# The front's adaLN weight blocks are loaded from GpSimd's queue instead of SyncE's

## The chip, the cores and the metric

The kernel runs on one core of a Trainium2 chip. The metric is the device time of one execution in microseconds (us). A core has TensorE (PE, with its weight loads PEld), VectorE (DVE), ScalarE (ACT), GpSimd (POOL) and SyncE (SP), which here only issues DMAs. Each engine takes its instructions in a fixed order and waits where one isn't ready.

## What is computed

One decoder layer over 256 tokens of width 2048. From a conditioning vector c a modulation is computed, a product of silu(c) with a weight of 2048 x 12288. It gives six vectors of 2048: shift, scale and gate for each of two sub-layers.

```
c_act = silu(c)
mod = c_act @ w_ada + b_ada
sh1, sc1, g1, sh2, sc2, g2 = split(mod, 6)
h = layer_norm(x) * (1 + sc1) + sh1
mix = token_mix(h, ...)          # one input projection w_in, two kinds of attention, w_o
x = layer_norm(alpha * x + g1 * mix)
h = layer_norm(x) * (1 + sc2) + sh2
ffn = peer(h, ...)               # queries w_pq, product keys, tables u and v
x = layer_norm(alpha * x + g2 * ffn)
```

## The kernel before, in words

Activations are kept transposed, 128 channels on the partitions, in 16 chunks. Weights come as pieces of 1 MB (128 partitions x 4 x 512 floats), 32 of w_in, then w_uq, w_uk, w_uv, 16 of w_o, 16 of w_pq, then the tables u and v. Some pieces are multiplied as they are, in float32 (L334); most are first split into a high and a low part: ACT casts the high part (L101), DVE subtracts it for the low part (L103), and PE makes three products (L140 to L142).

The modulation isn't a matmul. `ada` (L207) loads one block of w_ada, 1 MB, which holds the weights of 128 outputs, and DVE multiplies its two halves with the broadcast silu(c) and sums along the rows (L212, some 1.2 us each). The block's number j says which 128 of the 12288 outputs it gives. After a group of blocks `ada_bias` (L215) adds the two halves and the bias; ACT then applies shift and scale (L305, L740). The front, everything up to the table phase, takes 80 blocks this way:

- Eight blocks (shift and scale of the first four chunks) come before the first w_in piece can be finished. `group_start` (L359) loads the small w_kr tile (kw) and modulates the four chunks in two halves. The pieces of w_in for one group of four chunks are 8; `w_in_pieces` (L315) takes the first three together, first the products with the first half of the chunks for each piece, then those with the second half.
- Between the pieces of a group, `ada_in` (L350) takes the eight blocks of the next group. Buffers: two of `front` (tag "ada"), and the tiles xt0 and xt1 that held x. For the first group, the third and fourth block lie in the buffers of the pools early_a and early_b, the fifth and sixth in xt0 and xt1, which come free once PE has transposed the normalised x.
- w_in's own pieces use a ring of three buffers of `stream` and, by turns, the ones of early_a and early_b (RAW_RING, L324). So the third piece needs the fourth block's buffer and the fifth piece the third block's.
- The other 48 blocks (gate 1, shift 2, scale 2) are pulled from a generator, `ada_rest` (L244), at places written by hand (PULLS, PULL_WO, PULL_PQ; the rest at L792), and use the two buffers of `front` alone. The last ones feed `to_h2` (L736), which the last pieces of w_pq need.

The last 16 blocks (gate 2) are loaded in the table phase by code of their own, with SP's queue (g2w).

All DMAs are issued by SP, and SP's order is the program's: an issue that waits until its buffer is free holds back all that stand behind it. The order on the other engines is planned when the program is built, from the program's order and from what is ready; semaphores are added then. GpSimd does nothing after four memsets at the start.

Of the kernel before, what the change touches and what calls it, by code (L numbers as in the profile page):

```python
# [64 lines left out]
def tile_hybrid_peer_block(ctx: ExitStack, tc: tile.TileContext, a, out):  # L65
    nc = tc.nc
# [140 lines left out]
    def ada(pool, tag, bufs, j):  # L207

        w = pool.tile([P, D], F32, tag=tag, name=f"ada{j}", bufs=bufs).rearrange("p (z n) -> p z n", z=2)
        nc.sync.dma_start(w, a["w_ada"][j].rearrange("p (z n) -> p z n", z=2))  # L210
        for z in range(2):
            nc.vector.scalar_tensor_tensor(w[:, z, :], w[:, z, :], 1.0, cb[:, z * 1024:(z + 1) * 1024], op0=ALU.mult,  # L212
                                           op1=ALU.mult, accum_out=(modc, modh)[z][:, j:j + 1])
# [29 lines left out]
    with tc.tile_pool(name="front", bufs=1) as front:  # L243
        def ada_rest():  # L244
            for j in range(G1, SH2):
                ada(front, "ada", 2, j)
                yield
            ada_bias(G1, 16)
            for kg in range(4):
                for i in range(4):  # L250
                    for j0 in (SH2, SC2):
                        ada(front, "ada", 2, j0 + 4 * kg + i)
                        yield
                for j0 in (SH2, SC2):
                    ada_bias(j0 + 4 * kg, 4)
# [20 lines left out]
        with tc.tile_pool(name="mix", bufs=1) as mix, ExitStack() as attn_pool:  # L276
# [73 lines left out]
            def ada_in(kg, m):  # L350
                j = (SH1, SC1)[m % 2] + 4 * kg + m // 2
                where = (m // 2 % 2) if kg else (0, 2, 1, 0)[m // 2]
                if where == 0:
                    return ada(front, "ada", 2, j)
                if where == 1:
                    return ada(mix, f"xt{m % 2}", 1, j)
                return ada((early_a, early_b)[m % 2], "raw", 1, j)
# [273 lines left out]
        with tc.tile_pool(name="res", bufs=1) as res:  # L631
# [16 lines left out]
            for step in range(12):  # L648
# [6 lines left out]
                n = WO_ORDER[step][0]  # L655
# [145 lines left out]
    with tc.tile_pool(name="back", bufs=1) as back:  # L801
# [218 lines left out]
        with tc.tile_pool(name="val", bufs=1) as val:  # L1020
# [28 lines left out]
            for j, c in enumerate(V_ORDER):  # L1049
# [14 lines left out]
                if 2 <= j < 18:  # L1064
                    m = G2 + j - 2
                    w = g2w[:, j % 4, :].rearrange("p (z n) -> p z n", z=2)
# [36 lines left out]
            for th in range(2):  # L1103
# [18 lines left out]
                z = stream.tile([P, 4, 512], F32, tag="raw", name=f"fin_z{th}", bufs=3)  # L1122
# [79 lines left out]
```

## Time and profile before

| what | value |
|---|---|
| time, median of 3 runs | 2034.66 us (2030.68 to 2037.2) |
| profiled execution, its own time | 2032.56 us |
| its span, first to last instruction | 2030.5 us |
| mean granted TensorE clock over the span | 0.987 |
| PE, DVE, ACT, POOL busy | 1971.3, 1487.4, 1045.6, 0.2 us |

The profile is of one execution. A share of busy time is an average over stages. A wait is put down to what ended it. A DMA's time to landing runs from its issue until its data have arrived, and includes the time that it stands behind others in its queue.

### The profile page before, as it was taken

How to read it: one execution, taken by the hardware profiler on the slowest of the kernel's cores; microseconds unless marked ns; L12 is line 12 of the kernel's file. 1: busy time of each engine (PE TensorE's matmuls, PEld its weight loads, DVE VectorE, ACT ScalarE, POOL GpSimd, SP SyncE). 2: the span in 40 equal slices, each digit the busy share in tenths (PEclk: the TensorE clock that was granted, in tenths of full speed). 3: DMA queues.
4: the chain of work that ended last, by engine and by line, in shares of the span. 5: the costliest groups of instructions: out<-in, count | busy, mean ns of one | idle time of the engine just before them, and what ended most of it. 6: DMA issues, size and time to landing. Idle time of an engine off the chain costs nothing.

```text
span 2030.5 us, 26302 instructions
## 1 busy us (share of the span) xinstructions
PE 1971.3 (97%) x10119; PEld 1645.9 (81%) x10120; DVE 1487.4 (73%) x2334; ACT 1045.6 (51%) x1536; POOL 0.2 (0%) x4
## 2 busy tenths in 40 slices
PE   6999998999999999999999999999999999999997
PEld 4567676779988888888888888888888788888886
DVE  7588987888799777677777766686776666564457
ACT  2333457535545665677777765444444344444451
POOL 0000000000000000000000000000000000000000
PEclk7999998999999999999999999999999999999999
DMA  8887887877545676677777669989999988865552
GB/s 355 335 334 306 303 326 270 342 293 296 205 168 200 225 257 249 230 265 267 274 272 283 260 244 308 330 329 327 331 339 324 295 304 280 284 220 202 188 211 98
DMA packets 142829, 554.81 MB, mean 273 GB/s; under 512 B 10864, under 2 KB 77552, under 8 KB 84848
## 3 DMA queue, kind: packets, MB, share of 16 engines
q1 hardware_dynamic: 142704, 553.14, 74.0%
q8 instruction: 79, 1.29, 0.2%
q14 instruction: 46, 0.38, 0.1%
HBM read 502.76 MB, written 50.34 MB: 272 GB/s over the span
## 4 chain that ended last, share of the span: by engine, by line
PE 86%; DVE 8%; DMA 3%; ACT 2%; issue 1%; SPq 0%; DVEq 0%; ACTq 0%
PE u_ps L135 21%; PE u_ps L136 11%; PE v_ps L141 11%; PE v_ps L140 11%; PE v_ps L142 11%; PE win_ps L334 3%; PE win_ps L141 2%; DVE ada L212 2%; PE win_ps L142 2%; PE g_ps L967 2%; PE win_ps L140 1%; PE wo_ps L142 1%; PE wo_ps L141 1%; PE wo_ps L140 1%; PE wpq_ps L762 1%; DMA gl<-g_d 1%
## 5 line engine op out<-in xcount | busy, mean ns | idle before, releaser
L135 PE MATMUL u_ps<-act,hi_u 128*128 128x512 f32 x2048 | 719.7, 395 | 0.0
L136 PE MATMUL u_ps<-act,lo_u 128*128 128x256 f32 x2048 | 574.7, 281 | 0.5 <-DVE lo_u L103 0.4
L135 PEld LDWEIGHTS u_ps<-act,hi_u 128*128 128x128 f32 x2048 | 384.2, 188 | 86.1
L101 ACT CAST hi_v<-raw_v 128x1024 fp32r<-128x1024 f32 x244 | 256.9, 1054 | 332.0 <-PE v_ps L142 302.8
L103 DVE TENSOR_TENSOR lo_v<-raw_v,hi_v 128x1024 fp32r<-128x1024 f32 x244 | 296.0, 1222 | 177.9 <-ACT hi_v L101 177.9
L103 DVE TENSOR_TENSOR lo_u<-raw_u,hi_u 128x1024 fp32r<-128x1024 f32 x256 | 312.3, 1221 | 135.7 <-ACT hi_u L101 134.9
L136 PEld LDWEIGHTS u_ps<-act,lo_u 128*128 128x128 f32 x2048 | 386.8, 189 | 2.4 <-DVE lo_u L103 2.2
L141 PE MATMUL v_ps<-lo_v,whi 128*128 128x512 f32 x976 | 379.8, 389 | 1.8 <-DVE lo_v L103 1.8
L140 PE MATMUL v_ps<-hi_v,whi 128*128 128x512 f32 x976 | 379.9, 389 | 0.5 <-DVE W L823 0.5
L142 PE MATMUL v_ps<-hi_v,wlo 128*128 128x512 f32 x976 | 379.7, 389 | 0.0
L101 ACT CAST hi_u<-raw_u 128x1024 fp32r<-128x1024 f32 x256 | 267.4, 1048 | 174.2 <-PE u_ps L135 163.0
L141 PEld LDWEIGHTS v_ps<-lo_v,whi 128*128 128x128 f32 x976 | 183.2, 188 | 39.9 <-DVE lo_v L103 2.2
L140 PEld LDWEIGHTS v_ps<-hi_v,whi 128*128 128x128 f32 x976 | 183.2, 188 | 39.2 <-DVE W L823 1.2
L142 PEld LDWEIGHTS v_ps<-hi_v,wlo 128*128 128x128 f32 x976 | 183.2, 188 | 38.3
L212 DVE SCALAR_TENSOR_TENSOR ada<-ada,cb 128x1024 f32<-128x1024 f32 x160 | 191.0, 1218 | 8.1 <-DMA ada<-in_w_ada_dram 7.9
L962 DVE TENSOR_TENSOR o<-eq,gT 128x1024 fp32r<-128x1024 f32 x64 | 78.3, 1223 | 32.7 <-PE g_ps L967 32.7
L334 PE MATMUL win_ps<-raw_win,hmod 128*128 128x512 f32 x192 | 86.4, 605 | 1.2 <-ACT hmod L305 1.2
L824 ACT ACTIVATE W<-W 128x512 f32<-128x512 f32 x64 | 40.8, 637 | 70.3 <-DVE W L823 70.3
L970 ACT COPY stg<-g_ps 128x512 f32<-128x512 f32 x128 | 72.2, 623 | 0.0
L101 ACT CAST hi_win<-raw_win 128x1024 fp32r<-128x1024 f32 x40 | 40.7, 1049 | 60.7 <-DMA raw_win<-in_w_in_dram 30.6
L334 PEld LDWEIGHTS win_ps<-raw_win,hmod 128*128 128x128 f32 x192 | 36.6, 195 | 43.3 <-issue 41.2
L141 PE MATMUL win_ps<-lo_win,act 128*128 128x512 f32 x160 | 64.0, 400 | 5.8 <-DVE lo_win L103 5.6
(340 smaller groups left out, 2411.0 us busy)
## 6 DMA issues: line engine op xcount, KB each, us to landing
raw_u<-in_u_dram SPq DMA_DIRECT2D x128, 1024.0 KB, 5.3
raw_v<-in_v_dram SPq DMA_DIRECT2D x122, 1024.0 KB, 6.2
ada<-in_w_ada_dram SPq DMA_DIRECT2D x80, 1024.0 KB, 6.7
raw_win<-in_w_in_dram SPq DMA_DIRECT2D x32, 1024.0 KB, 8.8
g_d<-stg SPq DMA_DIRECT2D x16, 2048.0 KB, 7.2
gl<-g_d SPq DMA_DIRECT2D x32, 1024.0 KB, 10.0
raw_wo<-in_w_o_dram SPq DMA_DIRECT2D x16, 1024.0 KB, 6.9
g2w<-in_w_ada_dram SPq DMA_DIRECT2D x16, 1024.0 KB, 8.1
```

The costliest lines, as they stand in the source:

```text
L101: nc.scalar.copy(hi, raw[:, 2 * j:2 * j + 2, :])
L103: nc.vector.tensor_sub(lo, raw[:, 2 * j:2 * j + 2, :], hi.bitcast(F32))
L135: nc.tensor.matmul(pss[e], hi[:, i, es], act[:, k], start=first and j == 0 and i == 0, stop=False)
L136: nc.tensor.matmul(pss[e][:, 1], lo[:, i, es], act_hi[:, k, :], start=False, stop=last and j == 1 and i == 3)
L140: nc.tensor.matmul(o, sh, mh, start=start, stop=False)
L141: nc.tensor.matmul(o, sh, ml, start=False, stop=False)
L142: nc.tensor.matmul(o, sl, mh, start=False, stop=stop)
L212: nc.vector.scalar_tensor_tensor(w[:, z, :], w[:, z, :], 1.0, cb[:, z * 1024:(z + 1) * 1024], op0=ALU.mult, op1=ALU.mult, accum_out=(modc, ...
L334: nc.tensor.matmul(ps[th], act[:, i, ts], src[:, i, :], start=i == 0, stop=i == 3)
L824: nc.scalar.activation(ws, ws, AF.Gelu)
L962: nc.vector.tensor_mul(o2, eq.unsqueeze(2).broadcast_to(both), gT[:, four, :].bitcast(F32).unsqueeze(3).broadcast_to(both))
L970: nc.scalar.copy(stg[:, :, :, t:t + 2], ps.rearrange("p (t z i) -> p z i t", t=2, z=2))
```

## The change

`ada` issues its load from GpSimd's queue. Buffers, products, the places where blocks are taken, and every other load stay. It concerns the 80 blocks of the front.

```
@@ -207,7 +207,7 @@
     def ada(pool, tag, bufs, j):
 
         w = pool.tile([P, D], F32, tag=tag, name=f"ada{j}", bufs=bufs).rearrange("p (z n) -> p z n", z=2)
-        nc.sync.dma_start(w, a["w_ada"][j].rearrange("p (z n) -> p z n", z=2))
+        nc.gpsimd.dma_start(w, a["w_ada"][j].rearrange("p (z n) -> p z n", z=2))
         for z in range(2):
             nc.vector.scalar_tensor_tensor(w[:, z, :], w[:, z, :], 1.0, cb[:, z * 1024:(z + 1) * 1024], op0=ALU.mult,
                                            op1=ALU.mult, accum_out=(modc, modh)[z][:, j:j + 1])
```

## Rows read from the trace of the kernel before

**Rows 1.** The page's first part: busy us (share of the span) and instructions.

```profile
PE 1971.3 (97%) x10119; PEld 1645.9 (81%) x10120; DVE 1487.4 (73%) x2334; ACT 1045.6 (51%) x1536; POOL 0.2 (0%) x4
```

**Rows 2.** Busy us of PE, PEld, DVE, ACT, POOL by stretch; PEclk, DMA share, GB/s.

```profile
0.00:550.00 550.00, 506.11 (x2532) 393.24 (x2534) 448.18 (x944) 246.69 (x411) 0.20 (x4) 0.96 0.78 309
550.00:2030.50 1480.50, 1465.18 (x7590) 1252.67 (x7588) 1039.26 (x1392) 798.92 (x1125) 0.00 (x0) 1.00 0.73 260
```

**Rows 3.** PE's waits, 0 to 550 us: for whom, total us, times, longest us.

```profile
PE win_ps L141 <- DVE lo_win L103: 5.6, 4, 2.9
...
PE wpq_ps L140 <- ACT hi_wpq L101: 1.3, 1, 1.3
...
PE wpq_ps L142 <- DVE lo_wpq L103: 0.9, 2, 0.5
```

**Rows 4.** PE's timeline, 0 to 46 us: start, us, operation, [idle before it and releaser].

```profile
29.59 7.13 PE L334 MATMUL win_ps<-raw_win,hmod 128*128 128x512 f32 x16 [1.17 <-ACT hmod L305]
38.65 1.10 PE L310 MATMUL kr_ps<-kw,hmod 128*128 128x64 f32 x8 [1.93 <-DMA kw<-in_w_kr_dram]
42.03 1.12 PE L310 MATMUL kr_ps<-kw,hmod 128*128 128x64 f32 x4 [2.27 <-ACT hmod L305]
```

**Rows 5.** SP's longest wait by sum, and its issues of w_ada (ns min/median/max).

```profile
SPq L210 <- DVE ada L212: 131.9, 33, 11.6
...
L210 SPq DMA_DIRECT2D ada<-in_w_ada_dram x80: 327/328/835, 2.6 to 502.8; - x80
```

**Rows 6.** SP's timeline, 0 to 48 us.

```profile
24.79 4.94 SPq L210 DMA_DIRECT2D ada<-in_w_ada_dram  x4
29.77 0.73 SPq L362 DMA_DIRECT2D kw<-in_w_kr_dram  x1
30.60 0.40 SPq L85 DMA_DIRECT2D raw_win<-in_w_in_dram  x1
```

**Rows 7.** The tile ada, 28 to 30 us: its issues, and their time to landing.

```profile
L210 SPq DMA_DIRECT2D ada<-in_w_ada_dram x3: 328/423/424, 28.4 to 29.3; - x3
...
DMA to landing us min/median/max: 4.8/6.9/9.0
```

**Rows 8.** DVE's timeline, 0 to 42 us, and ACT's, 0 to 46 us.

```profile
27.21 0.08 DVE L212 DVE_READ_ACCUMULATOR ada<-ada,cb 128x1 f32 x1
...
39.72 1.22 DVE L212 SCALAR_TENSOR_TENSOR ada<-ada,cb 128x1024 f32<-128x1024 f32 x1
...
41.38 1.09 ACT L305 ACTIVATE hmod<-xnT,modc 128x256 f32<-128x256 f32 x2 [10.70 <-DVE modc L219]
```

**Rows 9.** SP's timeline, 466 to 520 us; issues at 477, 485 and 494 left out.

```profile
468.86 2.62 SPq L210 DMA_DIRECT2D ada<-in_w_ada_dram  x2
...
489.05 0.42 SPq L85 DMA_DIRECT2D raw_wpq<-in_w_pq_dram  x1
...
496.79 1.35 SPq L85 DMA_DIRECT2D raw_wpq<-in_w_pq_dram  x1
502.75 0.33 SPq L210 DMA_DIRECT2D ada<-in_w_ada_dram  x1
```

**Rows 10.** The tile xn, 0 to 30 us, and DVE's timeline there.

```profile
L284 SPq DMA_DIRECT2D xn<-in_x_dram x2: 424/428/432, 1.6 to 2.1; - x2
...
DMA to landing us min/median/max: 5.2/6.2/7.3
...
13.00 1.28 DVE L184 BATCH_NORM_STATS2 ln_st<-xn 128x6 f32<-128x512 f32 x2
```

**Rows 11.** The tile ada, 470 to 504 us: time to landing of its eight loads.

```profile
DMA to landing us min/median/max: 4.8/5.3/6.3
```

**Rows 12.** DVE's timeline at 509 us and ACT's at 511 us.

```profile
509.88 1.22 DVE L212 SCALAR_TENSOR_TENSOR ada<-ada,cb 128x1024 f32<-128x1024 f32 x1
...
511.53 2.08 ACT L740 ACTIVATE h<-xT,modc 128x256 f32<-128x256 f32 x4 [4.16 <-DVE modc L219]
```

More of the change, by code (lines that the diff above doesn't have):

```diff
@@ L209, in ada @@
         w = pool.tile([P, D], F32, tag=tag, name=f"ada{j}", bufs=bufs).rearrange("p (z n) -> p z n", z=2)
-        nc.sync.dma_start(w, a["w_ada"][j].rearrange("p (z n) -> p z n", z=2))
+        nc.gpsimd.dma_start(w, a["w_ada"][j].rearrange("p (z n) -> p z n", z=2))
         for z in range(2):
```

## Prediction

> **What bounds the kernel now.** I read the page's first part, then the busy time by stretch. TensorE (PE) is busy 1971.3 of 2030.5 us and GpSimd (POOL) does four memsets [rows 1]. The busy time by stretch says where PE's 59 idle us lie: 550.0 - 506.1 = 43.9 us in the first 550 us, the front, and 1480.5 - 1465.2 = 15.3 us in all the rest [rows 2]. Only the front holds the loads that move, so a gain has at most those 43.9 us to take from, while a loss has no such ceiling. Next I read PE's own waits in the front: the sort that a late weight piece makes is small, 5.6 us before the low-half product of w_in, 1.3 and 0.9 us before the w_pq pieces [rows 3]. The largest hole that can move lies at the start. PE runs the first halves of two w_in pieces from 29.59 us, is through by 36.72, and then waits 1.93 us for kw and 2.27 us for the second half of hmod, which starts the unbroken stream at 42.03 [rows 4].
>
> The SP timeline tells why loads look badly queued: its order is the program's, so a block of w_ada whose buffer is taken holds back the w_in or w_pq piece behind it. SP waited 131.9 us in 33 waits for VectorE (DVE) to finish with a block of w_ada [rows 5]. That is the queue's idle time and not PE's: PE lost the 7.8 us of [rows 3].
>
> **What the change removes.** 80 issues leave SP, 0.33 us each in the median, so 26 us of its issue time [rows 5]; no chain runs through that time, so it is worth nothing by itself. The head-of-line waits go as well. Where do they bind? Near 489 to 503 us: the w_pq loads at 489.05 and 496.79 each stand behind two blocks of w_ada whose issue waited for DVE [rows 9]. Loaded earlier, they save PE's 0.9 us before w_pq's low halves [rows 3]: -0.9. The 5.6 us at w_in's low halves I leave at 0, with bounds -5.6 and +4. Those pieces mostly wait for their own raw buffer, which PE frees, and DVE takes its products in an order fixed when the program is built, an order that will be planned anew; +4 is the same kind of stall nearly doubled.
>
> **What it adds, first place: the start.** The product that releases the stream is the eighth block of w_ada. SP issues four blocks from 24.79 on, then kw at 29.77, then a w_in piece at 30.60 [rows 6]. Three of the four go out at 28.4 to 29.3 us and land 4.8, 6.9 and 9.0 us later: the last at 38.3, so (9.0 + 0.9 - 4.8) / 2 = 2.5 us for each further MB [rows 7]. DVE's last product ends at 40.94, and ScalarE (ACT), idle for 10.70 us, starts hmod at 41.38 [rows 8]. This chain has no slack: landing, product, hmod, PE.
>
> Afterwards the w_in pieces no longer stand behind those blocks. The third needs the buffer that the fourth block leaves at 27.29 us, where its last product ends [rows 8]; the fourth has a free buffer of the three, the fifth one that the third block left. So SP asks for 3 MB from 27.3 us on, just as POOL asks for its last three blocks. No row shows two queues at once. If the blocks go first nothing is lost; if all three pieces go first, 3 x 2.5 = 7.5 us. I take 2.5 of the 3 pieces ahead of the last block, since SP asks a microsecond earlier: +6.2. PE uses part of that: the third piece's first half (half of the 7.13 us that two first halves took, so 3.6 us [rows 4]) is done while it waits. Net +2.6. The Trainium skill, page "DMA: Bandwidth & Descriptors", section "Queues, rings and completion order", says that each DMA engine takes turns between the queue rows that have work, packet by packet; by it the three blocks and three pieces would end together, the last block 7.5 us late, and the sum would be 1.3 us more.
>
> The same holds earlier for x. Its two halves land 5.2 and 7.3 us after issue because nothing is ahead of them, and DVE ends its statistics at 14.28 [rows 10]. With POOL's blocks beside them the second half can be up to 2 x 2.5 us later, at about 14.4; its four statistics (0.64 us each) would then end at 16.9, +2.7, unless DVE takes products first. Bounds 0 and +2.7, taken +1.3, the middle, since the order is planned anew. Start: +3.9.
>
> **Second place: the loop at the end of the front.** Before w_pq's last pieces the remaining nine blocks turn in two buffers: product done, buffer free, load, product. On one buffer five issues stand between 468.86 and 502.75 us, so 8.5 us apart [rows 9], of which 4.8 to 6.3 us is load [rows 11] and about 2.4 us product. The last product ends at 511.1, ACT waited 4.16 us for it before h, and PE waits behind that [rows 3, 12]. Five loads follow each other here, so every microsecond by which POOL's load is slower than SP's counts five times. POOL is in-order too, but behind its waiting load stand only other w_ada loads, and only DVE waits for them; DVE in turn has the low halves queued behind such a product.
>
> By how much POOL is slower the trace doesn't show, as POOL issues nothing. Below: the 0.33 us that SP's issue costs is saved, -0.33. Above: the spread of these loads under company, 6.3 - 4.8 = +1.5. I take +0.8, the nearest row being SP's slowest issue, 0.84 us [rows 5]: 5 x 0.8 = +4.0, bounds -1.6 and +7.5. The Trainium skill, same page, section "Specifications", gives a first byte of about 1 us by GpSimd's path and 0.6 by SP's; by that estimate the term would be 5 x 0.4 = +2.0 and the sum +5.0. Elsewhere in the front a block's product waits for DVE more than for its load, so I cost the 0.8 at nothing; without that cover it would be part of the +4 above.
>
> **Sum.** -0.9 + 3.9 + 4.0 = +7.0 us on the profiled execution's 2032.56 us, so 2039.6. The median shown is 2.1 us above that execution; set on the median, 2041.7. A measurement of this kernel can tell about 0.3%, 6.1 us, from no change, so the forecast is slower by just more than that.
>
> **Rivals.** *No change* (0.38). POOL's loads take as long as SP's and only the start's 2.6 us stay: 2034.66 + 2.6 = 2037. For it: PE is saturated between the two places. Against: the loop's five loads in series. The Trainium skill, same page, section "Issuing engines are not separate DMA queues", would even have 2034.66: all queues run on the same DMA engines, and another issuer saves only issue time. SP's 131.9 us of waiting speak neither for nor against that, since PE didn't wait there.
>
> *Faster* (0.16). Mechanism: pieces of w_in and w_pq always lie ready, DVE's products of w_ada slide into its idle stretches (it is busy 448 of 550 us [rows 2]), and all waits of [rows 3] go: -5.6 - 1.3 - 0.9 = -7.8, so 2026.9. It decides if POOL's extra time stays under about 0.2 us (5 x 0.2 = 1) and the blocks get ahead of the pieces at the start. For it: the w_pq pieces do stand behind w_ada. Against: the two gains of the loop hang on the block's product itself.
>
> *Much slower* (0.08, part of slower). If making a load takes POOL 3 us more, the loop alone gives +15 and DVE stalls in the 300 us before: 2034.66 + 15 + 6 = 2056.
>
> **How the numbers follow.** Slower 0.46, no change 0.38, faster 0.16. The likeliest case by itself spans 2041 to 2056: all upper bounds are 7.5 + 2.7 + 7.5 + 4 = +21.7, which need not all come together. The range over the cases reaches down through no change to the first part of faster, 2029, and up to 2055.
>
> **What would show it.** Right: POOL's w_ada loads land later than 4.8 us after issue even when alone; the eighth block lands after 38.3 us, at 43 or later, with w_in pieces in flight; PE's unbroken stream starts 2 to 6 us later than 42.03; the nine blocks at the end turn in 9 us or more and hmod's and h's waits on ACT grow. Wrong: the eighth block lands as before, or the cycle at the end is 8.5 us or less; PE's idle time in the front falls below 43.9 us; or idle time appears after 550 us, where I expect none.

## The result and the profile after

The changed kernel takes 2064.99 us (median of 4 runs, 2062.2 to 2067.31) against 2033.68 us of the kernel before on the same chip: 1.0152 times as long, 95% interval 1.0139 to 1.0164. That is 31 us slower where +7 was forecast, and outside the range. The profiled execution took 2064.46 us, with a span of 2062.6 us.

I read the profile after in the order of the prediction. First the page's part 1, then the busy time by stretch, the front's end moved on to 582 us (columns as in [rows 2]).

```profile
PE 1979.0 (96%) x10120; PEld 1649.2 (80%) x10120; DVE 1486.9 (72%) x2334; ACT 1045.0 (51%) x1536; POOL 43.2 (2%) x84
```

```profile
0.00:582.00 582.00, 513.95 (x2556) 398.85 (x2557) 450.50 (x963) 248.22 (x413) 43.24 (x84) 0.94 0.75 293
582.00:2062.60 1480.60, 1465.04 (x7567) 1250.38 (x7565) 1036.40 (x1373) 796.79 (x1124) 0.00 (x0) 1.00 0.73 260
```

The second stretch is as long as before ([rows 2]: 1480.5 us) because its start was set so: 582 us is 550 plus the 32.1 us by which the span grew. To compare the same work, both executions are cut at the first product of u, which comes at 596.14 us and before at 566.89 us, 29.2 us earlier. First the front after, then the front before:

```profile
0.00:596.14 596.14, 528.09 (x2675) 412.99 (x2676) 464.50 (x1029) 254.84 (x421) 43.24 (x84) 0.94 0.74 289
```

```profile
0.00:566.89 566.89, 523.00 (x2673) 410.13 (x2675) 464.94 (x1029) 254.76 (x421) 0.20 (x4) 0.96 0.77 304
```

So 29.2 of the 32.1 us were lost in the front: PE is idle 596.14 - 528.09 = 68.1 us there, 24.2 more than before, and busy 5.1 us more with the same work, at a mean granted clock of 0.94 against 0.96. The other 2.9 us come behind the front, where the executions differ by more than that without a cause in the edit (see the milestones below).

PE's timeline shows the two places where it waits most beyond before: the start (to be read beside [rows 4]) and the layer norm at 483 us, where the wait for xc was 2.07 us before.

```profile
26.50 3.73 PE L295 MATMUL xnT_ps<-ident,xn 128*128 128x128 f32 x16 [11.13 <-issue]
34.16 1.88 PE L295 MATMUL xnT_ps<-ident,xn 128*128 128x128 f32 x8 [3.92 <-DVE xn L190]
40.90 1.97 PE L295 MATMUL xnT_ps<-ident,xn 128*128 128x128 f32 x8 [4.87 <-ACT xnT L296]
...
55.35 0.66 PE L310 MATMUL kr_ps<-kw,hmod 128*128 128x64 f32 x4 [2.27 <-ACT hmod L305]
...
482.98 1.97 PE L722 MATMUL h_ps<-ident,xc 128*128 128x128 f32 x8 [5.90 <-ACT xc L719]
```

The unbroken stream starts at 55.35 instead of 42.03 us, 13.3 us late. Before it, ACT's timeline has something that the kernel before doesn't have: two casts of a w_in piece stand among the copies of xnT and wait 7.52 us for that piece.

```profile
30.27 0.59 ACT L296 COPY xnT<-xnT_ps 128x512 f32<-128x512 f32 x1 [0.27 <-PE xnT_ps L295]
38.37 1.99 ACT L101 CAST hi_win<-raw_win 128x1024 fp32r<-128x1024 f32 x2 [7.52 <-DMA raw_win<-in_w_in_dram]
40.27 1.07 ACT L296 COPY xnT<-xnT_ps 128x512 f32<-128x512 f32 x2
...
54.70 1.09 ACT L305 ACTIVATE hmod<-xnT,modc 128x256 f32<-128x256 f32 x2 [9.57 <-DVE modc L219]
```

So the order of the instructions changed too, on every engine. The edit is one word, but a DMA on another queue is another instruction to the planner, and it planned the whole front anew. The loads themselves changed as follows (the tile xn, 0 to 20 us; the tile ada, 0 to 560 us).

```profile
L284 SPq DMA_DIRECT2D xn<-in_x_dram x2: 424/428/432, 1.7 to 2.1; - x2
DMA to landing us min/median/max: 8.4/10.7/12.9
```

```profile
DMA to landing us min/median/max: 5.0/7.5/20.5
```

x lands 3.2 and 5.6 us later than in [rows 10]. The quickest block lands 5.0 us after its issue against 4.7 in the same view of before, so POOL's queue by itself adds about 0.3 us, not 0.8.

Three theories, then. **Order**: the loss is the planner's new order. **Queue**: it is what POOL's queue does, whatever the order, and inside it either its latency or the **precedence** that SP's single queue gave: while a block waited for its buffer, the pieces behind it were held, and when both were free the block went first.

### The profile page after: what moved, and what is told of

The parts are those of the page before. It is cut to its first block, busy times and chain, and to the rows that moved or that the text cites. A ratio compares the mean times of both kernels' runs of the same rounds, so it can differ in the third digit from the quotient of the medians.

```text
span 2062.6 us, 26396 instructions
## 1 busy us (share of the span) xinstructions
PE 1979.0 (96%) x10120; PEld 1649.2 (80%) x10120; DVE 1486.9 (72%) x2334; ACT 1045.0 (51%) x1536; POOL 43.2 (2%) x84
## 3 DMA queue, kind: packets, MB, share of 16 engines
q0 software_dynamic: 11520, 83.89, 10.5%
## 4 chain that ended last, share of the span: by engine, by line
PE 70%; issue 8%; DVE 6%; DMA 5%; ACT 0%; SPq 0%; POOL 0%; DVEq 0%; ACTq 0%; POOLq 0%
PE u_ps L135 22%; PE u_ps L136 11%; PE v_ps L141 10%; PE v_ps L142 10%; PE v_ps L140 10%; DMA ada<-in_w_ada_dram 2%; DMA gl<-g_d 2%; PE g_ps L967 1%; DVE ada L212 1%; DVE lo_u L103 1%; PE wpq_ps L142 1%; DMA raw_v<-in_v_dram 1%; PE wpq_ps L141 1%; PE wpq_ps L140 1%; DVE lo_v L103 1%
## 5 line engine op out<-in xcount | busy, mean ns | idle before, releaser
L140 PE MATMUL win_ps<-hi_win,act 128*128 128x512 f32 x160 | 65.2, 410 | 6.5 <-ACT hi_win L101 5.4
```

What stands on the lines that cost most here:

```text
L140: nc.tensor.matmul(o, sh, mh, start=start, stop=False)
```

## The experiments

In all runs but two (e3 and e4), the order in which the engines' instructions stand was pinned. A table of the finished order of one kernel is written into another, and each instruction gets an ordering edge, without a wait, to the one ahead of it on its engine. What the table leaves out is planned. So the queue and the order can be changed one without the other:

```
         tile_hybrid_peer_block(tc, aps, out)
+        _in_order(tc, _ORDER)
...
+def _in_order(tc, text):
...
+            prev = last.get(ins.engine)
+            if prev is not None:
+                tc.add_manual_dep(ins, prev.name, mybir.DependencyInfo(
+                    mybir.DependencyClass.NoSync, mybir.DependencyReason.DATA), reason="in_order")
+            last[ins.engine] = ins
```

Three milestones on PE say where a run loses. They are steadier than the total: from the first u product to the end, where the instructions are the same in all runs, the profiled executions take from 1463.6 us (before) to 1471.7 us (e6). But they too are read from one execution each. The start of e6, e7 and e11, whose loads and order there are those of before, comes 0.8 to 1.0 us earlier than before, and e10 is 2.6 us ahead of the change already at 400 us, in front of the stretch that it edits. A difference of 1 to 3 us between two traces is therefore not shown to be an effect. The milestones are in us, in the profiled executions, and their delay against before; the last column is the median of the runs against that of before on the same chip.

| run | second half of group 0 | layer norm's first transposes | first u product | median, ratio (95%) |
|---|---|---|---|---|
| before | 42.0 | 455.8 | 566.9 | |
| the change | +13.3 | +27.2 | +29.2 | 1.0152 (1.0139 to 1.0164) |
| e1: POOL, old order | +11.7 | +13.5 | +21.4 | 1.0097 (1.0078 to 1.0117) |
| e2: SP, new order | +26.6 | +60.0 | +58.8 | 1.0278 (1.0257 to 1.0299) |
| e3: first 8 on SP, planned | +9.6 | +29.7 | +31.9 | 1.0190 (1.0166 to 1.0215) |
| e4: first 8 on POOL, planned | +15.4 | +18.0 | +17.4 | 1.0081 (1.0061 to 1.0100) |
| e5: blocks and pieces on POOL | +3.3 | +6.5 | +11.6 | 1.0060 (1.0042 to 1.0077) |
| e6: 72 on POOL, old order | -1.0 | +1.7 | +9.2 | 1.0052 (1.0035 to 1.0069) |
| e7: last 9 on POOL, old order | -1.0 | +0.8 | +7.8 | 1.0041 (1.0026 to 1.0057) |
| e8: SP, hand order | -2.9 | -2.3 | -2.2 | 0.9988 (0.9975 to 1.0002) |
| e9: the whole front on POOL | +1.1 | +4.3 | +4.4 | 1.0045 (1.0031 to 1.0059) |
| e10: the change, one stretch swapped | +14.0 | +19.6 | +26.7 | 1.0168 (1.0151 to 1.0185) |
| e11: w_pq pieces on POOL, old order | -0.8 | +0.3 | +1.5 | 1.0033 (1.0020 to 1.0047) |
| e12: SP, second hand order | -3.7 | -3.4 | -5.0 | 0.9983 (0.9971 to 0.9995) |

### e1 and e2: the queue without the order, the order without the queue

e1 is the changed kernel with the order of before on PE, DVE, ACT, SP and POOL. e2 is the kernel before with the order of the change on PE, DVE and ACT; SP's order was left to the planner.

> All 80 front loads go out on POOL's queue, but every engine's instructions stand in the order that they had before (the order of the kernel before is written into the program as ordering edges without waits; POOL takes the loads in the relative order that SP had them). Theory A (the loss is the re-planned order: work that waits for a load stands ahead of work that is needed first): the queue alone costs what the prediction gave it, so 2034 to 2044 us. Theory B (the loss is the queue: transfers of two queues share the DMA engines, and each load lands later): the time stays at that of the change, 2058 to 2067 us. Theory C (half and half): 2046 to 2054 us.

> The mirror of the run with the old order: all loads go out on SP, as before, but PE, DVE and ACT have their instructions in the order that the changed kernel has (SP's own order is left to the planner). Theory A (the order): the loss is here without any POOL load, 2055 to 2070 us. Theory B (the queue): as before, 2030 to 2040 us. Theory C: 2042 to 2052 us.

e1: 2055.56 us (before 2034.62), so 21 of the change's 31 us come with the old order: mostly the queue. e2: 2092.14 us, 57 slower, more than any theory gave. The two don't add up, so the new order is no constant price: it costs 9 us where it was planned for (2064.99 - 2055.56) and 57 with loads on SP, in an order of SP's that was new as well. In e2 PE's timeline shows how such an order loses: the normalised x stands on DVE behind products of blocks, xnT's copies on ACT behind casts.

```profile
37.94 1.94 PE L295 MATMUL xnT_ps<-ident,xn 128*128 128x128 f32 x8 [11.22 <-DVE xn L190]
52.44 1.97 PE L295 MATMUL xnT_ps<-ident,xn 128*128 128x128 f32 x8 [12.56 <-ACT xnT L296]
```

In e1 ACT has no cast among the copies, yet the start is 11.7 us late all the same. The casts that caught the eye in the profile after are therefore not needed for a late start; what they cost in the change itself wasn't measured. Four views of e1 give its cause: POOL's timeline, SP's, and the loads issued at 30 to 33 us with their time to landing, of the tile ada and of raw_win.

```profile
28.33 0.53 POOL L210 DMA_DIRECT2D ada<-in_w_ada_dram  x1 [24.86 <-PE xnT_ps L295]
31.45 1.57 POOL L210 DMA_DIRECT2D ada<-in_w_ada_dram  x3 [2.60 <-DVE modc L219]
```

```profile
30.88 1.28 SPq L85 DMA_DIRECT2D raw_win<-in_w_in_dram  x3
```

```profile
L210 POOL DMA_DIRECT2D ada<-in_w_ada_dram x3: 527/527/530, 31.5 to 32.5; - x3
...
DMA to landing us min/median/max: 10.5/14.9/17.7
```

```profile
L85 SPq DMA_DIRECT2D raw_win<-in_w_in_dram x3: 327/376/432, 30.9 to 31.8; - x3
DMA to landing us min/median/max: 7.3/11.9/16.6
```

Issue plus landing time gives the moments: pieces at 38.2, 43.2 and 48.3 us, blocks at 41.9, 46.9 and 50.2. They land strictly by turns. Three blocks that took 4.8 to 9.0 us with nothing ahead of them but each other [rows 7] take 10.5 to 17.7, and PE, through with what it had, waits for the last (PE's timeline):

```profile
39.30 1.00 PE L310 MATMUL kr_ps<-kw,hmod 128*128 128x64 f32 x8
53.72 1.12 PE L310 MATMUL kr_ps<-kw,hmod 128*128 128x64 f32 x4 [13.42 <-ACT hmod L305]
```

### e3 and e4: parts of the change, planned anew

```
-        nc.gpsimd.dma_start(w, a["w_ada"][j].rearrange("p (z n) -> p z n", z=2))
+        (nc.gpsimd if next(ada_count) >= 8 else nc.sync).dma_start(w, a["w_ada"][j].rearrange("p (z n) -> p z n", z=2))
```

`ada_count` counts the blocks from 0. e4 has `< 8` in place of `>= 8`. Both are left to the planner.

> The changed kernel with the first group's 8 blocks back on SP and the other 72 on POOL; the planner orders it anew. In the trace of the change the PE stream starts 13.3 us late behind the sixth of these blocks. If that start is a loss that nothing gives back, 2050 to 2054 us (13 less than the change). If the later stages only take over the wait (the DMA engines being full until 150 us), 2060 to 2066 us.

> The kernel before with only the first group's 8 blocks on POOL, ordered anew by the planner. If the start costs what the trace of the change shows there, 13 us more than before: 2044 to 2050 us. If the loss comes from the whole mixture of the two queues, 2032 to 2040 us.

e3: 2072.05 us, slower than the whole change; e4: 2052.75 us, above its first range. As parts they would sum to 37 + 18 = 55 us, against 31 for the whole: a part of the change that the planner orders anew isn't a part of the change. After this I pinned the order.

### e5, e6 and e7: parts with the order pinned

e5 puts the w_in, w_kr, latent, w_o and early w_pq pieces on POOL's queue too, in SP's old order:

```
-        nc.sync.dma_start(raw, src)
+        front_load[0](raw, src)
...
+    front_load = [nc.gpsimd.dma_start]
...
+        front_load[0] = nc.sync.dma_start
         def w_tile(c, name):
```

e6 is e3's edit with the old order, e7 the same with `>= 71`.

> With the order of before on every engine, the w_in, w_kr, w_uq/w_uk/w_uv, w_o and w_pq pieces follow the 80 blocks onto POOL's queue, all in the order that SP had them; SP keeps x, cols, the constants and the stores. So one queue again, but POOL's. Theory P (what costs in the run with the old order is the lost precedence: pieces that SP held behind blocks now start with or ahead of them): the 8 us of the last loop go, and of the 11 us of the start only x's lateness stays (x still shares with the first blocks, 3 to 4 us): 2036 to 2042 us. Theory L (POOL's queue is slow in itself, its issue takes 0.53 us against 0.33 and more loads now pay for it): 2055 us or more.

> The old order on every engine, the first group's 8 blocks on SP, the other 72 on POOL. The run with all 80 on POOL in the old order lost 11 us by the second half of the first group, 2 between there and 456 us and 8 in the last loop. If these parts stand for themselves, the start's 11 us go and the rest stays: 2042 to 2047 us. If the blocks of the second group, now alone on POOL, overtake the first group's on SP (theory P at another place), the start stays late: 2050 to 2058 us.

> The old order, and only the last 9 blocks (those loaded during the w_pq stage) on POOL. Theory P: SP, no longer held by a block that waits for its buffer, issues three w_pq pieces at once and the blocks land behind them: 8 us, 2040 to 2044 us. The prediction's reading of this loop (the pieces come earlier, -0.9, and each of some 5 loads that end a wait costs POOL's added latency, here measured as 0.3 us, so +1.5): 2033 to 2036 us.

e6: 2047.43 us, just above the range of "parts stand for themselves", and in the trace the start's delay is gone while the loop's is there (+7.5). e7: 2044.92 us, a little above the first range, with only nine loads moved, and +7.0 us between layer norm and u, where e1 has +7.9: the loop stands for itself. The loss is that of theory precedence and not of the prediction's reading of the loop; e11 below narrows it. In e7 the last block's product now holds ACT 16.41 us where it held it 4.16 [rows 12]:

```profile
519.35 2.08 ACT L740 ACTIVATE h<-xT,modc 128x256 f32<-128x256 f32 x4 [16.41 <-DVE modc L219]
```

e5: 2048.82 us, between its theories. The start fits precedence (+3.3, expected 3 to 4), and the three blocks, loaded at 31.6 to 32.6 us with no piece between them, land as in [rows 7]:

```profile
DMA to landing us min/median/max: 5.1/7.0/9.0
```

But the loop still lost 5.1. The edit does less than the expectation says: the later w_pq pieces stayed on SP, and two of them go out at 498.77 and 507.67 us among the last blocks. So e5's loop still had two queues; e9 takes that up.

### e9 and e11: one queue of POOL's, and the opposite split

In e9 every DMA of the front is POOL's, in SP's old order. e11 leaves all blocks on SP and gives the later w_pq pieces to POOL:

```
-        nc.sync.dma_start(raw, src)
+        (nc.gpsimd if name[:3] == "wpq" and name not in ("wpq0_0", "wpq1_0") else nc.sync).dma_start(raw, src)
```

> The old order, and every DMA of the front (x, cols, constants, blocks, all pieces, the stores of x1) on POOL's queue in the order that SP had them; SP has only the loads of the u and v stages and their stores. Nothing shares with anything that SP held back, so what is left is POOL's own latency, 0.3 us a load that ends a wait and 0.3 us from a release to an issue. Theory P (lost precedence): start 1 to 3 us late, last loop 2 to 4 us longer, 2037 to 2042 us. Theory L (POOL's queue is slow in itself): the last loop still loses 5 us or more and the start 4 or more, 2045 us or more.

> The opposite split: all 80 blocks stay on SP, and the 13 later w_pq pieces go on POOL, the old order on every engine. If precedence is the cause it doesn't matter which of the two goes to POOL: the pieces are no longer held behind blocks that wait for their buffers, three start at once, and the loop is 7 to 9 us longer as in the run with the last 9 blocks on POOL: 2041 to 2045 us. If POOL's latency for the blocks were the cause, nothing is lost here: 2033 to 2036 us.

e9: 2043.8 us, between the ranges, but by its places it is precedence: the start is 1.1 us late and the last loop 0.1 longer. (The profiled execution, 2038.34 us, is the fastest of its six.) POOL's timeline has the three blocks, kw and the piece in SP's old order, and the blocks' landings are those of [rows 7] within 0.2 us:

```profile
29.49 1.57 POOL L210 DMA_DIRECT2D ada<-in_w_ada_dram  x3 [3.13 <-PE xnT_ps L295]
31.05 0.54 POOL L362 DMA_DIRECT2D kw<-in_w_kr_dram  x1
31.58 0.53 POOL L85 DMA_DIRECT2D raw_win<-in_w_in_dram  x1
```

```profile
DMA to landing us min/median/max: 5.0/7.0/9.0
```

The other 3.2 us come at one place. DVE waits 3.54 us for a block (1.10 before), behind it stands the split that frees a buffer for ACT's copies qr_lt, and PE waits for these, 4.94 us against 1.47 before (DVE's timeline, then PE's):

```profile
378.62 1.22 DVE L212 SCALAR_TENSOR_TENSOR ada<-ada,cb 128x1024 f32<-128x1024 f32 x1 [3.54 <-DMA ada<-in_w_ada_dram]
```

```profile
383.13 2.29 PE L236 MATMUL g_ps<-g_dg,ones 128*128 128x128 f32 x9 [4.94 <-ACT qr_lt L485]
```

e11: 2040.79 against 2033.11 us, by its time a hair under the range of precedence, but not by its mechanism: in the trace the loop is 1.2 us longer, not 7 to 9. Pieces that are no longer held don't cost 7 us by themselves. Compare the loads at 476 to 477.5 us (tile ada, then raw_wpq), e7 first:

```profile
L210 POOL DMA_DIRECT2D ada<-in_w_ada_dram x1: 530/530/530, 477.1 to 477.1; - x1
DMA to landing us min/median/max: 10.4/10.4/10.4
```

```profile
L85 SPq DMA_DIRECT2D raw_wpq<-in_w_pq_dram x1: 328/328/328, 476.7 to 476.7; - x1
DMA to landing us min/median/max: 9.7/9.7/9.7
```

and e11:

```profile
L210 SPq DMA_DIRECT2D ada<-in_w_ada_dram x1: 328/328/328, 476.0 to 476.0; - x1
DMA to landing us min/median/max: 5.1/5.1/5.1
```

```profile
L85 POOL DMA_DIRECT2D raw_wpq<-in_w_pq_dram x1: 530/530/530, 476.4 to 476.4; - x1
DMA to landing us min/median/max: 9.0/9.0/9.0
```

In e7 the block goes out 0.4 us behind a piece and lands after 10.4 us; in e11 0.4 us ahead of it and after 5.1. Being asked for first isn't the whole of it: in e7 the piece was first and still took 9.7 us. Order and queue change together between the two runs, so which of them gives the 5 us isn't shown. In these traces the loop's loss needs both: one slow queue for all costs 0.1 (e9), pieces let loose beside blocks on the quick queue 1.2 (e11), pieces let loose beside blocks on the slow one 7.0 (e7; 7.5 in e6, 7.9 in e1).

The medians of e9 and e11 are above what their fronts explain (4.4 us are 0.22%, 1.5 us 0.07%) by 6 us each, and so is that of e10 below by 7 (2066.75 - 2033.11 = 33.6, of which its front has 26.7). The three ran on one chip and have little else in common, so the edits hardly explain this. It stays open.

### e10: one stretch of the new order put back

e10 has the change's own order but for 20 instructions of ACT and 54 of DVE round the layer norm, which stand among themselves as before; on DVE for example

```
-L644 TENSOR_TENSOR wo_t_1_3251<-wo_ps_1_3202,g1b 128x512
 L703 TENSOR_TENSOR mv_x_0_3184<-sums_3177 128x2
...
+L644 TENSOR_TENSOR wo_t_1_3251<-wo_ps_1_3202,g1b 128x512
```

> The changed kernel with its own order written down on every engine, but 20 neighbouring instructions of ACT and 54 of DVE round the layer norm's first half (the sq, mv_x, rs_r chain, a residual and two casts of a w_pq piece) in the order among themselves that they had before. In the trace of the change this stretch has PE's wait for xc at 5.90 us against 2.07 before, because the residual that waits for PE and a cast that waits for a buffer stand ahead of the chain. If re-planning is what the old-order run does not lose, this one swap gives back the difference, 3 to 4 us: 2060 to 2062 us, and PE's wait for xc is 2.1 us. If later waits take it over, 2064 to 2067 us.

PE's wait for xc falls from 5.90 to 2.29 us, and the layer norm's transposes come 7.6 us earlier against before than in the change (+19.6 for +27.2). Of these, 2.6 us are there already at 400 us, ahead of the stretch; the other 5.0 are what the planner's order cost there.

```profile
475.39 1.45 PE L722 MATMUL h_ps<-ident,xc 128*128 128x128 f32 x8 [2.29 <-ACT xc L719]
```

But the total, 2066.75 us, is that of the change, and at the first u product only 2.5 us are left (+26.7 for +29.2), what it had ahead of the stretch: the last loop takes 7.1 us more than before, as in e1 and e7, where in the change it takes 2.0 more. So the second theory holds: later waits took it over. That PE came to the loop late enough in the change for the blocks to be less in its way is the likely reason, but no run shows it.

### e8 and e12: the order alone, as a gain

No load is on POOL here. e8 moves two blocks in SP's order of the first group (and their products on DVE likewise), e12 also one later block's products into a gap on DVE, for which its pull stands earlier in the program.

```
+L210 DMA ada_269<-in_w_ada_dram 128x2048
+L210 DMA ada_273<-in_w_ada_dram 128x2048
 L210 DMA ada_261<-in_w_ada_dram 128x2048
 L210 DMA ada_265<-in_w_ada_dram 128x2048
-L210 DMA ada_269<-in_w_ada_dram 128x2048
-L210 DMA ada_273<-in_w_ada_dram 128x2048
```

```
-PULL_PQ = (4, 4, 0, 0, 2, 0, 0, 5, 6, 0, 2, 0)
+PULL_PQ = (3, 4, 0, 0, 2, 0, 0, 5, 6, 0, 2, 0)
...
+                ada_pull(1)
                 for n in range(3):
                     half_piece(n, 0)
```

> All loads on SP, no POOL load; the order of before but for the first group: blocks m6 and m7 (whose buffers are free at 16.7 and 19.7 us) are issued ahead of m4 and m5 (whose buffers are free at 24.8 and 28.5), and their products moved likewise on DVE. If order in the queue is the lever, the last of the eight products ends some 2.5 us earlier and the DMA stream with it: 2030 to 2033 us beside a before of 2034, hardly more than can be measured. If the DMA engines are the bound whatever stands in the queue: 2033 to 2036 us.

> All loads on SP, the order of before with two hand-made moves. The first is that of the earlier hand-ordered run (blocks m6 and m7 ahead of m4 and m5 in the first group; there the trace had the rest of the front 2.2 us earlier). The second: one block's two products, which stood on DVE at 466.5 us behind the layer norm although the block had landed long before, fill the 2.5 us at 461.1 us in which DVE waits for ACT's sq; the next block's load then goes out some 5 us earlier into DMA engines that are idle there. If the order of loads and products is the lever, the w_pq stage ends 4 to 5 us earlier than before and the time is 2028 to 2031 us beside a before of 2034. If the last loop is bound by the pieces instead, only the first move's 2 us: 2031 to 2034 us.

e8: 2034.88 against 2035.38 us; the front is 2.2 us shorter, near the 2.5 expected but within what two traces differ by, and the total can't be told from no change. e12: 2031.22 against 2035.17 us, ratio 0.9983 (0.9971 to 0.9995). The front is 5.0 us shorter, as the first theory has it; the total lies just above its range. It is the one kernel here that beats both, by 0.2%. DVE's and SP's timelines show the second move: the product at 457.63 us, formerly behind the layer norm, and the next block's load right after it.

```profile
457.63 1.22 DVE L212 SCALAR_TENSOR_TENSOR ada<-ada,cb 128x1024 f32<-128x1024 f32 x1
```

```profile
460.03 5.40 SPq L210 DMA_DIRECT2D ada<-in_w_ada_dram  x2
```

## Why the prediction was wrong

The direction was right and the first place, the start, was the right one; the size was off by a factor of more than four. The prediction also counts PE's idle time alone, while 5.1 of the front's 29.2 us are the same work taking PE longer at a lower granted clock. By its own steps:

**The start, +3.9 forecast, +11.7 measured with the old order (+13.3 in the change).** The runs split the 11.7. POOL's own latency is 1.1 us (e9), no more than two traces differ by. x sharing with the first blocks is another 2.2 (e5 less e9, 3.3 - 1.1); I took 1.3 and had 2.7 as bound. The pieces let loose are 8.4 (e1 less e5, 11.7 - 3.3), where I had +2.6. e1's loads alone say the same: the last block goes out 3.2 us later than before (32.5 for 29.3) and takes 8.7 us longer. Two steps under that 2.6 failed. "2.5 of the 3 pieces ahead" gave 6.2, while the three blocks end 17.7 - 9.0 = 8.7 us slower. The Trainium skill, page "DMA: Bandwidth & Descriptors", section "Queues, rings and completion order", says that the engines take turns between queues that have work; the trace of e1 agrees, with landings strictly by turns, and its 7.5 us would have been the better figure. And the credit of 3.6 us for PE working meanwhile never came: in e1 PE sits idle 13.42 us, because in its order nothing else stands ahead of the second half. The split is that of the old order. In the change itself the three blocks go out at 43.17 us only, after a wait for DVE, and the second of them, whose product releases PE's second half, lands at 52.1; how much of that is order and how much queue no run separates (POOL's timeline of the change, then DVE's).

```profile
43.17 1.57 POOL L210 DMA_DIRECT2D ada<-in_w_ada_dram  x3 [9.04 <-DVE modc L219]
```

```profile
52.14 1.23 DVE L212 SCALAR_TENSOR_TENSOR ada<-ada,cb 128x1024 f32<-128x1024 f32 x1 [1.38 <-DMA ada<-in_w_ada_dram]
```

**The head-of-line waits, -0.9 forecast.** This is the step whose sign was wrong. I counted SP's waits as a cost and their removal as a small gain. The pieces did come earlier: e7 issues its next two at 476.68 and 479.58 us, where before they went out at 479.89 and 489.05 us. But in the last loop the blocks end the chain, and beside pieces that were no longer held they came late: +7.0 with the blocks on POOL's queue (e7), 1.2 with the pieces there instead (e11).

**The loop, 5 x 0.8 = +4.0 forecast.** The latency is 0.3 us (5.0 against 4.7), and alone it costs the loop 0.1 us (e9): POOL's issue of 0.53 us against 0.33 is real but disappears in the cycle. The loop did lose 7.9 us (e1), for the reason of the paragraph above. The Trainium skill, same page, section "Specifications", gives a difference of 0.4 us for the first byte, near the 0.3 measured; its section "Issuing engines are not separate DMA queues" says that the loads of all issuers run on the same engines and interleave, and that another issuer saves only issue time. The interleaving is what e1 shows; that nothing but issue time would change, as I read it, fails here by e1's 21 us, since the order in which the engines are asked isn't kept.

**The middle, 0 forecast, bounds -5.6 and +4.** With the old order it is 13.5 - 11.7 = +1.8, inside. In the change it is 27.2 - 13.3 = +13.9. I named that DVE's order "will be planned anew", set the term at 0 and priced its bound as one w_in stall doubled. It is every engine's order, through 550 us, and this is the term that failed in the middle. Its net price in the front is 29.2 - 21.4 = +7.8 us (2064.99 - 2055.56 = +9.4 on the medians): 1.6 us at the start (13.3 - 11.7) and 12 in the middle (13.9 - 1.8) are lost, 6 are given back in the loop (7.9 in e1, 29.2 - 27.2 = 2.0 in the change). Which instructions cost the middle's 12 is shown for 5.0 us at the layer norm alone (e10); for the rest it stays open.

**After 550 us** nothing was expected, and hardly anything is there: behind the first u product PE is idle no longer than before (15.6 against 15.3 us), though busy 2.6 us longer.

Of the signs listed, the late block came (50.2 us in e1, 52.1 in the change), and the later stream, by more than the 2 to 6 us named. Of ACT's waits the one for h grew (7.34 us for 4.16); the one for hmod did in e1 (19.65 for 10.70) but not in the change (9.57). The rival "much slower" had the nearest number, 2056 us, but not by its mechanism: making a load takes POOL 0.2 us more, not 3. "Faster" named two conditions, POOL's extra time under 0.2 us and the blocks ahead of the pieces at the start; neither came (0.3 us, and landings by turns). The pieces let loose, its source of gain, did the harm.

## What to carry to other kernels

A queue in which one transfer waits and holds others is also a priority list. Before giving some of its loads a queue of their own, look at each place where both queues will have work and ask which load ends the chain there; if it is the one that was first in line, splitting the queue can take its place away. And where a planner sets the order of instructions, pin the old order to see what the edit itself does, since a new order can cost as much as the edit and hide or double it.

## What was not expected of the hardware

Six loads of 1 MB asked of SP and POOL within 1.7 us landed strictly by turns, so that a block that was last of three on its queue took 17.7 us instead of 9.0. An issue takes POOL 0.53 us in the median, where SP's median is 0.33. And a block asked for on SP's queue 0.4 us ahead of a piece on POOL's landed after 5.1 us (e11), while one asked for on POOL's queue 0.4 us behind a piece on SP's took 10.4, and that piece 9.7 (e7).
